# One-hot tiles of a gate expansion laid out as [token pair, key, 2] instead of [key, 8 tokens] in a one-core decoder trunk

## The chip, the cores and the metric

The kernel runs on one core of a Trainium2 chip. The metric is the device time of one execution in microseconds (us), from the first instruction to the last. The engines have short names in the rows: PE is the TensorE matmul, PEld its weight load, DVE the VectorE, ACT the ScalarE, POOL the GpSimd, SP the SyncE, which issues most of the transfers. Instructions of one engine run in the program's order; engines wait for each other by semaphores.

## What is computed

One decoder layer on 1024 tokens of width 1024, with 16 meta tokens in front: a convolution module beside latent attention, and then a mixer in which each of 8 heads picks, for each token, 16 of 16384 experts by a product of two key sets of 128 keys each. The mixer is what matters here:

```python
sv, si = lax.top_k(s, K)
cand = sv[:, :, 0, :, None] + sv[:, :, 1, None, :]
cidx = si[:, :, 0, :, None] * N_KEYS + si[:, :, 1, None, :]
top_s, sel = lax.top_k(cand.reshape(C, PEER_HEADS, K * K), K)
eidx = jnp.take_along_axis(cidx.reshape(C, PEER_HEADS, K * K), sel, axis=-1)
g = jax.nn.softmax(top_s, axis=-1)
u = u_tab[eidx]
act = jax.nn.gelu(jnp.einsum('chkd,cd->chk', u, xb).astype(jnp.float32), approximate=False)
w = (g * act).astype(xb.dtype)
return jnp.einsum('chk,chkd->cd', w, v_tab[eidx])
```

An expert's number is `i1 * 128 + i2`, with `i1` and `i2` the two keys. Each token has 8 x 16 = 128 (head, pick) pairs with a gate each.

## The kernel before

The tokens are cut into 8 chunks of 128. Input product, convolution and attention come first. For the mixer, four chunks (`GATHER`) fetch the rows of their experts by indirect transfers, and four (`DENSE`) go through all 16384 experts by matmul. A **gather step** of the first kind is 4 fetches `ug` (L687, issued by POOL) of 512 KB each into one of 3 buffers, and for each a DVE product with the tokens, `ujunk` (L690); of the second kind 4 fetches `vg` (L713) into 7 buffers, and 8 matmuls `gv` (L717).

The dense chunks need their gates as a table over all experts, `g_d`, in DRAM. `expand` (L738 to L764) makes it. For one dense chunk, the 128 (head, pick) pairs lie in the partitions, and the tile `gd` holds for each of 128 tokens the gate's high part (row 0) and low part (row 1), `i1` (row 2) and `i2` (row 3), all in 16-bit floats. The work goes in 4 blocks of 32 tokens, each block in 4 **batches** of 8 tokens (`TH`), so 64 batches in all. A batch has, on DVE, two comparisons of `gd` with the key numbers `io`, which give the one-hot tiles `two` (L749) and `one` (L750), the product `ah` (L751), and in batches 0 and 2 of a block also the product `al` (L752); in batches 1 and 3 POOL does `al` (`ALP`). Then PE does for each of the 8 tokens two matmuls (L756 with `ah`, L757 with `al`), each of which loads `two` as 128 x 128 weights and streams 128 columns, and adds them up in PSUM in `pg`. ACT copies `pg` out into `st` (L759), and SP writes a full `st` to `g_d` (L763). There is one buffer for `one`, and there are two each for `two`, `ah` and `al`.

What stands in memory: a tile of 128 x 128 x 8 two-byte elements with the token innermost. One token's 128 keys, which a matmul reads as its weights or its columns, therefore lie 16 bytes apart:

```python
one, two, ah, al = [ex.tile([P, NK, TH], F16, name=f"{n}{c}_{q}_{r0}", tag=n, bufs=b)
                    for n, b in (("one", 1), ("two", 2), ("ah", 2), ("al", 2))]
V.tensor_tensor(two, io, col(3), op=OP.is_equal)
PE.matmul(pg[:, k], two[:, :, r + k], ah[:, :, r + k], start=True, stop=False)
```

The order of the work: the code emits parts in the order of the string `ORDER`, and a scheduler then orders every engine's instructions by its own model of time. `E0` to `E3`, the expansions of the four dense chunks, run among the last selects (`S4`), the last product with `w_out` and the last query scores (`C4`), the transposed dense input (`N0`), the first three dense blocks (`U3`) and gather steps. After them comes the dense part (`dense`), with matmuls `pa` and `pv` (L178), in 32-bit format, 128 x 128 weights and 512 columns each. The last 128 gather steps run beside the dense part.

Of the kernel before, what the change touches and what calls it, by code (L numbers as in the profile page):

```python
# [16 lines left out]
F16 = mybir.dt.float16  # L17
# [3 lines left out]
OP = mybir.AluOpType  # L21
# [4 lines left out]
P = 128  # L26
D = 1024
KD = D // P
S = 1024
# [16 lines left out]
BIG = 3.0e38  # L46
# Pairs (a0, na, b0, nb) of sorted key scores that can be among the 16 (the first four: the 8) largest sums.
BLOCKS = [(0, 1, 0, 8), (1, 1, 0, 4), (2, 2, 0, 2), (4, 4, 0, 1),
# [8 lines left out]
WT = 512  # L57
# Emission order after the first chunk: B attention, C mix and query scores, S select, T turn of a token set;
# E gate expansion of a dense chunk, N transposed dense input, U dense blocks ahead, G gather steps, D the rest;
# X and Y hand the attention's and the mix's memory on.  # L60
ORDER = "B1 C1 S1 B2 C2 T1 S2 B3 C3 T2 S3 B4 X0 C4 T3 E0 E1 Y0 S4 T4 E2 N0 E3 U3 G32 D0"
# [21 lines left out]
def trunk_kernel(ctx, tc, x, meta, g_mix, w_ab, w_lat, g_q, w_uq, g_kv, w_ukv, conv_w, conv_b,  # L83
# [53 lines left out]
    def rsqrt(ms, name):  # L137
        """(ms + EPS) ** -0.5 of a [p, width] mean square, in place."""
        p, w = ms.shape
        G.tensor_tensor(ms, ms, pow_c[:p, 0, :w], op=OP.add)  # L140
        G.tensor_tensor(ms, ms, pow_c[:p, 1, :w], op=OP.pow)
        return ms
# [15 lines left out]
    def split_w(pool, ap, shape, name, bufs, eng):  # L158
        """Weight tile [P, nk, n] as an exact sum of two float32r parts."""
        nk, n = shape  # L160
        raw = pool.tile([P, WT], F32, name=name + "r", tag="wraw", bufs=4)
        hi = pool.tile([P, WT], F32R, name=name + "h", tag="whi", bufs=bufs)
        lo = pool.tile([P, WT], F32R, name=name + "l", tag="wlo", bufs=bufs)
        r, hh, ll = [t[:, :nk * n].rearrange("p (k n) -> p k n", n=n) for t in (raw, hi, lo)]
        nc.sync.dma_start(r, ap)
        A.activation(hh, r, AF.Copy)
        eng.tensor_tensor(ll, r, hh.bitcast(F32), op=OP.subtract)
        return hh, ll
# [11 lines left out]
    def to_T(src, m, XT, c0, k0=0, nk=KD, bank=bank):  # L180
        """Transposes rows src [m, nk * P] into the split pair XT at columns c0.."""
        for b in range(0, nk, 4):
# [18 lines left out]
    def phase_a():  # L201
        """Input norm, w_in product, conv module and the latent attention's projections; a generator that
        yields once the first chunk's part and everything that needs the transposed input is emitted."""
        ax_ctx, aw_ctx = ExitStack(), ExitStack()
# [35 lines left out]
        def project(j):  # L240
# [17 lines left out]
            def rope(dst, src, nh):  # L258
                """dst, src [m, nh, DR]"""
                co = cst[:m, None, :HF].broadcast_to([m, nh, HF])  # L260
# [11 lines left out]
            def headsT(src, dst_d, name):  # L272
                """src [m, H, DQ] -> dst_d [DQ, H, m]"""
                ht = pj.tile([DQ, H, P], F32, name=name, tag="hT", bufs=2)
                for b in range(2):
                    tq = bank("tq", tag="ap")
                    for q in range(4):
                        transpose_to(tq[:DQ, q * P:q * P + m], src[:m, 4 * b + q], m)
                    A.activation(ht[:, 4 * b:4 * b + 4, :m], tq.rearrange("p (k t) -> p k t", t=P)[:DQ, :, :m], AF.Copy)
                nc.scalar.dma_start(dst_d, ht[:, :, :m])  # L280
# [24 lines left out]
        def conv_v(b, c0, n, acc):  # L305
            """acc [P, n]: channel block b of the conv at tokens c0.."""
            for k in range(CK):
# [6 lines left out]
        def conv_g(b, c0, n, acc, pool):  # L314
            """The same with the products on ScalarE and the sums, in two chains, on GpSimd."""
            acc2 = pool.tile([P, n], F32, name=f"odd{b}_{c0}", tag=f"odd{n}", bufs=1)
# [97 lines left out]
    def attend_first():  # L414
        """Attention of the first chunk, four heads at a time."""
        qt = bp.tile([DQ, H, P], F32, name="qt0")
# [135 lines left out]
    def mix_out(si, MT):  # L552
# [5 lines left out]
        for nn in range(4):  # L558
            w = [load_w(cp, w_out[nn, :, 2 * kk:2 * kk + 2], (2, 256), f"wo{si}_{nn}_{kk}") for kk in range(4)]
            for j in range(nt):  # L560
# [4 lines left out]
                V.tensor_tensor(hv, hv, pb, op=OP.add)  # L565
# [1 line left out]
        NT = cp.tile([P, KD, dim.nw * P], F32, name=f"nt{si}", tag="mt", bufs=2)  # L567
        for j in range(nt):
# [5 lines left out]
            to_T(hs[j], P, NT, j * P)  # L574
# [1 line left out]
        sv = [sel.tile([P, H, 2, TK], F32, name=f"sv{si}_{j}", tag="sv", bufs=dim.nw) for j in range(nt)]  # L576
# [79 lines left out]
    def turn(c):  # L656
        """Expert indices (and gates) of chunk c with the (head, k) pairs in the partitions."""
        ef, g = picks[c]
# [17 lines left out]
    def gather_u(c):  # L676
        """Rows of u_tab against the tokens of chunk c; yields after every 4 (head, k) pairs."""
        g, ei = chunks[c][:2]
# [16 lines left out]
    def gather_v(c):  # L695
        """Weighted rows of v_tab for the tokens of chunk c; yields after every 4 tokens."""
        g, ei, eT = chunks[c]
# [40 lines left out]
    def expand(ci):  # L738
        """Dense gates of the DENSE tokens: g_d[i1 // NG, i2, t // TG, (i1 % NG, t % TG)]."""
        c = DENSE[ci]  # L740
        t = chunks[c]
        for q in range(P // TG):
            st = [ex.tile([P, NK // 2, TG], F32, name=f"st{c}_{q}_{i}", tag="st", bufs=STB) for i in range(2)]
            for r0 in range(0, TG, TH):
                def col(r):
                    return t[:, r, None, q * TG + r0:q * TG + r0 + TH].broadcast_to([P, NK, TH])
                one, two, ah, al = [ex.tile([P, NK, TH], F16, name=f"{n}{c}_{q}_{r0}", tag=n, bufs=b)
                                    for n, b in (("one", 1), ("two", 2), ("ah", 2), ("al", 2))]
                V.tensor_tensor(two, io, col(3), op=OP.is_equal)  # L749
                V.tensor_tensor(one, io, col(2), op=OP.is_equal)  # L750
                V.tensor_tensor(ah, one, col(0), op=OP.mult)  # L751
                (G if r0 // TH in ALP else V).tensor_tensor(al, one, col(1), op=OP.mult)  # L752
                for r in range(0, TH, 4):
                    pg = bank(f"pg{c}_{q}_{r0}_{r}", (P, 4, NK), "bs"[r // 4 % 2])
                    for k in range(4):
                        PE.matmul(pg[:, k], two[:, :, r + k], ah[:, :, r + k], start=True, stop=False)  # L756
                        PE.matmul(pg[:, k], two[:, :, r + k], al[:, :, r + k], start=False, stop=True)  # L757
                    for i in range(2):
# [128 lines left out]
    for step in ORDER.split():  # L887
# [11 lines left out]
        elif step[0] == "X":  # L899
            bp_ctx.close()  # L900
            ex = ex_ctx.enter_context(tc.tile_pool(name="ex", bufs=1, side="right", **RW))
            io = ex.tile([P, NK, TH], F16, name="io")
            G.iota(io, pattern=[[1, NK], [0, TH]], base=0, channel_multiplier=0, allow_small_or_imprecise_dtypes=True)
        elif step[0] == "Y":
# [22 lines left out]
def _layout(i):  # L927
# [3 lines left out]
    def blocks(w, n):  # L931
        """[D, M] -> [M / n, P, D / P, n]"""
        d, m = w.shape
        return c(w.reshape(d // P, P, m // n, n).transpose(2, 1, 0, 3))
# [43 lines left out]
```

## Time and profile before

| What | Value |
|---|---|
| Median of 3 runs | 3082.31 us (3082.04 to 3083.99) |
| Profiled execution, first to last instruction (its span, which is its time here) | 3090.9 us |
| Mean granted TensorE clock | 0.902 of full |
| Busy: PE / PEld / DVE / ACT / POOL | 2742.6 / 1995.1 / 2160.4 / 1022.9 / 1567.2 us |
| Moved by transfers | 858.36 MB, mean 278 GB/s |
| First and last matmul `pg` start at | 963.6 and 1435.6 us |

The profiled execution lies 8.6 us above the median. The chain of waits follows the work that ended last back to the start, and its shares say on what the end depended. A matmul's end in the rows is modelled, so the distance between the starts of two matmuls in a row says what one costs, and not its length. [...]

### The profile page before, as it was taken

How to read it: one execution, taken by the hardware profiler on the slowest of the kernel's cores; microseconds unless marked ns; L12 is line 12 of the kernel's file. 1: busy time of each engine (PE TensorE's matmuls, PEld its weight loads, DVE VectorE, ACT ScalarE, POOL GpSimd, SP SyncE). 2: the span in 40 equal slices, each digit the busy share in tenths (PEclk: the TensorE clock that was granted, in tenths of full speed). 3: DMA queues.
4: the chain of work that ended last, by engine and by line, in shares of the span. 5: the costliest groups of instructions: out<-in, count | busy, mean ns of one | idle time of the engine just before them, and what ended most of it. 6: DMA issues, size and time to landing. Idle time of an engine off the chain costs nothing.

```text
span 3090.9 us, 40498 instructions
## 1 busy us (share of the span) xinstructions
PE 2742.6 (89%) x13295; PEld 1995.1 (65%) x13295; DVE 2160.4 (70%) x4917; ACT 1022.9 (33%) x2200; POOL 1567.2 (51%) x1608
## 2 busy tenths in 40 slices
PE   7778578888876997887999899999999999999997
PEld 6765456766644654444877767777777777776664
DVE  4788957989988789855778776666666665653333
ACT  6445335443421333333322222322222222332222
POOL 5885443535568356654333354554455445434444
PEclk9898769988897776656999999999999999999999
DMA  4124689887788777879888899999999999988986
GB/s 156 33 59 146 215 271 314 271 260 227 242 312 295 244 262 237 276 253 304 291 281 292 286 353 336 334 355 339 333 354 335 345 324 351 333 322 313 325 305 225
DMA packets 372563, 858.36 MB, mean 278 GB/s; under 512 B 37952, under 2 KB 134400, under 8 KB 368256
## 3 DMA queue, kind: packets, MB, share of 16 engines
q0 software_dynamic: 147456, 536.94, 50.0%
q1 hardware_dynamic: 216528, 295.68, 28.4%
q10 hardware_dynamic: 8368, 23.15, 2.0%
q8 instruction: 105, 1.72, 0.2%
q14 instruction: 106, 0.87, 0.1%
HBM read 798.92 MB, written 56.71 MB: 277 GB/s over the span
## 4 chain that ended last, share of the span: by engine, by line
PE 58%; DVE 14%; DMA 11%; issue 5%; POOL 3%; ACT 1%; SPq 0%; another core or an unknown queue 0%; POOLq 0%; ACTq 0%; DVEq 0%
PE pa L178 19%; PE pv L178 19%; DMA ug<-in_dram,ei 8%; PE gv L717 7%; DVE ujunk L690 3%; PE pg L756 3%; PE pg L757 3%; PE q L583 3%; DVE ef L638 2%; DVE eq L636 1%; PE po L521 1%; POOL vg L713 1%; PE sp L493 1%; PE op L563 1%; DMA vg<-in_dram,eT 1%
## 5 line engine op out<-in xcount | busy, mean ns | idle before, releaser
L713 POOL DMA_INDIRECT vg<-in_dram,eT x512 | 556.6, 1087 | 682.7 <-PE gv L717 544.0
L687 POOL DMA_INDIRECT ug<-in_dram,ei x512 | 540.9, 1056 | 624.6 <-DVE ujunk L690 341.1
L690 DVE SCALAR_TENSOR_TENSOR ujunk<-ug,xn 128x1024 bf16<-128x1024 f32 x512 | 631.7, 1234 | 144.3 <-DMA ug<-in_dram,ei 137.0
L830 DVE TENSOR_TENSOR acc<-acc,pv 128x512 f32<-128x512 f32 x256 | 171.8, 684 | 213.2 <-PE pv L178 193.3
L717 PE MATMUL gv<-vg,wd 128*32 128x512 f32 x2048 | 278.0, 663 | 25.6 <-DMA vg<-in_dram,eT 25.6
L756 PE MATMUL pg<-ah,two 128*128 128x128 f16 x512 | 205.6, 414 | 41.7 <-DVE ah L751 39.6
L178 PE MATMUL pv<-v_0h,wh 128*128 128x512 f32 x512 | 203.1, 400 | 26.4 <-ACT wh L816 18.2
L759 ACT ACTIVATE st<-pg 128x256 f32<-128x256 f32 x256 | 140.0, 652 | 253.7 <-PE pg L757 228.1
L757 PE MATMUL pg<-al,two 128*128 128x128 f16 x512 | 204.7, 412 | 17.2 <-POOL al L752 15.8
L178 PE MATMUL pa<-xdh,u_1l 128*128 128x512 f32 x512 | 202.4, 395 | 2.4 <-DVE u_1l L779 2.4
L178 PE MATMUL pa<-xdh,u_0l 128*128 128x512 f32 x512 | 203.0, 396 | 0.2 <-DVE u_0l L779 0.2
L178 PE MATMUL pv<-v_1l,wh 128*128 128x512 f32 x512 | 200.5, 393 | 2.7 <-DVE v_1l L779 2.7
L178 PE MATMUL pa<-xdh,u_0h 128*128 128x512 f32 x512 | 202.9, 396 | 0.0
L178 PE MATMUL pa<-xdl,u_0h 128*128 128x512 f32 x512 | 202.1, 395 | 0.0
L178 PE MATMUL pa<-xdl,u_1h 128*128 128x512 f32 x512 | 201.6, 394 | 0.0
L178 PE MATMUL pv<-v_0l,wh 128*128 128x512 f32 x512 | 201.3, 396 | 0.0
L178 PE MATMUL pa<-xdh,u_1h 128*128 128x512 f32 x512 | 200.7, 392 | 0.0
L778 ACT ACTIVATE u_1h<-u_1r 128x512 fp32r<-128x512 f32 x128 | 80.7, 631 | 360.2 <-PE pa L178 268.9
L178 PE MATMUL pv<-v_1h,wl 128*128 128x512 f32 x512 | 199.5, 391 | 0.0
L178 PE MATMUL pv<-v_1h,wh 128*128 128x512 f32 x512 | 195.9, 394 | 1.8 <-DVE acc L830 1.8
L178 PE MATMUL pv<-v_0h,wl 128*128 128x512 f32 x512 | 194.0, 395 | 0.3 <-DVE wl L817 0.3
L778 ACT ACTIVATE u_0h<-u_0r 128x512 fp32r<-128x512 f32 x128 | 80.8, 631 | 310.6 <-PE pa L178 240.9
(449 smaller groups left out, 5932.1 us busy)
## 6 DMA issues: line engine op xcount, KB each, us to landing
g_d<-st SPq DMA_DIRECT2D x32, 1024.0 KB
u_0r<-in_dram SPq DMA_DIRECT2D x128, 256.0 KB
u_1r<-in_dram SPq DMA_DIRECT2D x128, 256.0 KB
gt<-g_d SPq DMA_DIRECT2D x32, 1024.0 KB
v_0r<-in_dram SPq DMA_DIRECT2D x128, 256.0 KB
v_1r<-in_dram SPq DMA_DIRECT2D x128, 256.0 KB
wo<-in_dram SPq DMA_DIRECT2D x80, 256.0 KB
wq<-in_dram SPq DMA_DIRECT2D x80, 256.0 KB
```

Source lines behind the costliest of these rows:

```text
L178: PE.matmul(dst, l, r, start=first and j == 0, stop=last and j == 2)
L583: PE.matmul(pb[:, :n], w[:, k], NT[:, kk + k, :n], start=kk + k == 0, stop=kk + k == KD - 1)
L638: V.tensor_reduce(e[:, h:h + HB, ks], pr.rearrange("p h c k -> p h k c"), axis=AX.X, op=OP.add)
L687: G.indirect_dma_start(out=ug, out_offset=None, in_=u_tab, in_offset=bass.IndirectOffsetOnAxis(ap=ei[:, j:j + 1], axis=0))
L690: V.scalar_tensor_tensor(junk, ug, 1.0, xn, op0=OP.mult, op1=OP.mult, accum_out=dots[:, j:j + 1])
L713: G.indirect_dma_start(out=vg[j], out_offset=None, in_=v_tab, in_offset=bass.IndirectOffsetOnAxis(ap=eT[:, t:t + 1], axis=0))
L717: PE.matmul(acc[32 * j:32 * j + 32, 512 * n:512 * n + 512], w[:, j, 32 * i:32 * i + 32], vg[j][:, 512 * n:512 * n + 512], start=q == 0 and ...
L756: PE.matmul(pg[:, k], two[:, :, r + k], ah[:, :, r + k], start=True, stop=False)
L757: PE.matmul(pg[:, k], two[:, :, r + k], al[:, :, r + k], start=False, stop=True)
L759: A.activation(st[i][:, :, r0 + r:r0 + r + 4].rearrange("p a b -> p b a"), pg[:, :, i * NK // 2:(i + 1) * NK // 2], AF.Copy, scale=1.0 / G ...
L778: A.activation(hi, raw, AF.Copy)
L830: V.tensor_tensor(a, a, pv, op=OP.add)
```

## The change

The four tiles get the shape [128, 4, 128, 2]: token pair, key, and the token within the pair innermost. One token's 128 keys now lie 4 bytes apart, not 16. `io` shrinks from [128, 8] to [128, 2] per partition and is read again for each pair, and the column operand `col` is read as runs of 2 elements, each run 128 times over, where it was a run of 8 read 128 times. The counts of instructions, their element counts and types, the matmuls' shapes, PSUM tiles, copies and transfers stay. Comments and docstrings are dropped as well.

```diff
             for r0 in range(0, TG, TH):
+                sh = [P, TH // 2, NK, 2]
+
                 def col(r):
-                    return t[:, r, None, q * TG + r0:q * TG + r0 + TH].broadcast_to([P, NK, TH])
-                one, two, ah, al = [ex.tile([P, NK, TH], F16, name=f"{n}{c}_{q}_{r0}", tag=n, bufs=b)
+                    cv = t[:, r, q * TG + r0:q * TG + r0 + TH].rearrange("p (a b) -> p a b", b=2)
+                    return cv[:, :, None, :].broadcast_to(sh)
+                one, two, ah, al = [ex.tile(sh, F16, name=f"{n}{c}_{q}_{r0}", tag=n, bufs=b)
                                     for n, b in (("one", 1), ("two", 2), ("ah", 2), ("al", 2))]
-                V.tensor_tensor(two, io, col(3), op=OP.is_equal)
-                V.tensor_tensor(one, io, col(2), op=OP.is_equal)
+                V.tensor_tensor(two, io[:, None].broadcast_to(sh), col(3), op=OP.is_equal)
+                V.tensor_tensor(one, io[:, None].broadcast_to(sh), col(2), op=OP.is_equal)
                 V.tensor_tensor(ah, one, col(0), op=OP.mult)
                 (G if r0 // TH in ALP else V).tensor_tensor(al, one, col(1), op=OP.mult)
...
-                        PE.matmul(pg[:, k], two[:, :, r + k], ah[:, :, r + k], start=True, stop=False)
-                        PE.matmul(pg[:, k], two[:, :, r + k], al[:, :, r + k], start=False, stop=True)
+                        a, b = divmod(r + k, 2)
+                        PE.matmul(pg[:, k], two[:, a, :, b], ah[:, a, :, b], start=True, stop=False)
+                        PE.matmul(pg[:, k], two[:, a, :, b], al[:, a, :, b], start=False, stop=True)
...
-            io = ex.tile([P, NK, TH], F16, name="io")
-            G.iota(io, pattern=[[1, NK], [0, TH]], base=0, channel_multiplier=0, allow_small_or_imprecise_dtypes=True)
+            io = ex.tile([P, NK, 2], F16, name="io")
+            G.iota(io, pattern=[[1, NK], [0, 2]], base=0, channel_multiplier=0, allow_small_or_imprecise_dtypes=True)
```

The scheduler also sets instructions of the expansions, and of what runs among them, in a somewhat different order from the start of `E0` on; ahead of that the order stays. In the changed file the lines of the batch are L752 to L755 and L760, L761. Two places are shown. The first is POOL in the last expansion, from the product `al` of block 1 (its last batch) to that of block 2; in the names, `al_2_8` is block 2 from token 8 on, and the numbers at the end are buffers. Before:

```order
L752 TENSOR_TENSOR al_1_24_11052<-one_1_24_11049,gd_10258 128x1024
L752 TENSOR_TENSOR al_2_8_11116<-one_2_8_11113,gd_10258 128x1024
L687 DMA ug_84_14090<-in_dram,ei_4618 128x1024
L687 DMA ug_85_14094<-in_dram,ei_4618 128x1024
L713 DMA vg_126_15046<-in_dram,eT_2889 128x1024
L713 DMA vg_31_15278<-in_dram,eT_2889 128x1024
L713 DMA vg_63_15280<-in_dram,eT_2889 128x1024
L713 DMA vg_95_15282<-in_dram,eT_2889 128x1024
L752 TENSOR_TENSOR al_2_24_11176<-one_2_24_11173,gd_10258 128x1024
```

And with the change:

```order
L755 TENSOR_TENSOR al_1_24_11052<-one_1_24_11049,gd_10258 128x1024
L687 DMA ug_85_14094<-in_dram,ei_4618 128x1024
L755 TENSOR_TENSOR al_2_8_11116<-one_2_8_11113,gd_10258 128x1024
L687 DMA ug_86_14098<-in_dram,ei_4618 128x1024
L713 DMA vg_127_15284<-in_dram,eT_2889 128x1024
L713 DMA vg_0_15373<-in_dram,eT_5632 128x1024
L687 DMA ug_87_14102<-in_dram,ei_4618 128x1024
L713 DMA vg_32_15375<-in_dram,eT_5632 128x1024
L755 TENSOR_TENSOR al_2_24_11176<-one_2_24_11173,gd_10258 128x1024
```

The fetches stand between the products in another order, and the stretch holds three fetches of each kind where it held two `ug` and four `vg`; by the last `al` of all, one `ug` and four `vg` more have been issued than before.

The second place is DVE at the same point, from the batch that starts at token 24 of block 1 into block 2. Before:

```order
L750 TENSOR_TENSOR one_1_24_11049<-io,gd_10258 128x1024
L751 TENSOR_TENSOR ah_1_24_11051<-one_1_24_11049,gd_10258 128x1024
L750 TENSOR_TENSOR one_2_0_11083<-io,gd_10258 128x1024
L749 TENSOR_TENSOR two_2_0_11084<-io,gd_10258 128x1024
L751 TENSOR_TENSOR ah_2_0_11085<-one_2_0_11083,gd_10258 128x1024
L752 TENSOR_TENSOR al_2_0_11086<-one_2_0_11083,gd_10258 128x1024
L749 TENSOR_TENSOR two_2_8_11114<-io,gd_10258 128x1024
L750 TENSOR_TENSOR one_2_8_11113<-io,gd_10258 128x1024
L690 SCALAR_TENSOR_TENSOR ujunk,dots_12008<-ug_81_14018,xn_12006 128x1024
L749 TENSOR_TENSOR two_2_16_11144<-io,gd_10258 128x1024
```

And with the change:

```order
L753 TENSOR_TENSOR one_1_24_11049<-io,gd_10258 128x1024
L754 TENSOR_TENSOR ah_1_24_11051<-one_1_24_11049,gd_10258 128x1024
L752 TENSOR_TENSOR two_1_24_11050<-io,gd_10258 128x1024
L690 SCALAR_TENSOR_TENSOR ujunk,dots_12008<-ug_82_14022,xn_12006 128x1024
L753 TENSOR_TENSOR one_2_0_11083<-io,gd_10258 128x1024
L754 TENSOR_TENSOR ah_2_0_11085<-one_2_0_11083,gd_10258 128x1024
L752 TENSOR_TENSOR two_2_0_11084<-io,gd_10258 128x1024
L755 TENSOR_TENSOR al_2_0_11086<-one_2_0_11083,gd_10258 128x1024
L752 TENSOR_TENSOR two_2_8_11114<-io,gd_10258 128x1024
L753 TENSOR_TENSOR one_2_8_11113<-io,gd_10258 128x1024
```

A product with a fetched row, `ujunk`, moves up by some five places, and `two` stands behind `ah` in two batches; the rule that `one` of the next batch follows the last reader of `one` on POOL or DVE stays.

## Rows read from the trace of the kernel before

**Rows 1.** The page: the span, and PE's clock in 40 slices of 77 us (tenths).

```profile
span 3090.9 us, 40498 instructions
...
PEclk9898769988897776656999999999999999999999
```

**Rows 2.** The page: the two groups of matmuls of the expansion (busy us, mean ns, idle before).

```profile
L756 PE MATMUL pg<-ah,two 128*128 128x128 f16 x512 | 205.6, 414 | 41.7 <-DVE ah L751 39.6
...
L757 PE MATMUL pg<-al,two 128*128 128x128 f16 x512 | 204.7, 412 | 17.2 <-POOL al L752 15.8
```

**Rows 3.** Busy time by stretch: start:end, length, PE, PEld, DVE, ACT, POOL, clock, DMA share, GB/s.

```profile
955.00:1110.00 155.00, 139.29 (x584) 90.01 (x586) 117.04 (x328) 46.19 (x93) 85.58 (x85) 0.80 0.76 259
1110.00:1260.00 150.00, 119.14 (x510) 68.69 (x503) 141.98 (x414) 49.63 (x94) 98.86 (x107) 0.70 0.75 249
1260.00:1436.00 176.00, 151.33 (x643) 78.86 (x644) 114.11 (x169) 68.76 (x127) 103.08 (x78) 0.57 0.84 276
1436.00:1810.00 374.00, 336.49 (x1441) 265.67 (x1441) 281.92 (x472) 104.73 (x185) 139.58 (x128) 0.96 0.86 296
1810.00:3090.00 1280.00, 1260.57 (x6188) 910.46 (x6186) 732.79 (x1175) 354.35 (x593) 601.71 (x563) 1.00 0.91 329
```

**Rows 4.** The chain of waits by line, in the first, second and third stretch of rows 3.

```profile
by line: PE q L583 19.4%; PE pg L756 18.3%; PE pg L757 18.2%; issue 5.9%; PE gv L717 4.9%; PE s L592 4.9%; POOL vg L713 4.1%; DVE ef L638 3.8%; POOL ep L637 3.6%; POOL cidx L619 3.5%; DVE ujunk L690 3.3%; DVE eq L636 2.7%; PE tp L156 2.2%; 
by line: PE pa L178 14.5%; PE pg L756 10.3%; PE pg L757 9.4%; DVE eq L636 7.6%; DVE ef L638 5.8%; DVE ujunk L690 4.6%; PE gv L717 4.5%; DMA xd<-xn_d 3.7%; DVE two L749 3.6%; DVE ah L751 3.6%; issue 3.3%; PE q L583 3.1%; DVE one L750 2.8%; D
by line: PE pg L757 24.6%; PE pg L756 23.6%; PE gv L717 14.1%; issue 11.0%; POOL al L752 7.2%; POOL vg L713 6.8%; DVE ah L751 4.7%; DVE two L749 2.0%; DVE ujunk L690 1.9%; POOL ug L687 1.9%; DVE one L750 1.4%; POOL ep L637 0.5%; ACT st L759
```

**Rows 5.** PE in order of time: `pg` around 1016 us, where 1.00 was granted.

```profile
1016.06 0.41 PE L757 MATMUL pg<-al,two 128*128 128x128 f16 x1
1016.29 0.41 PE L756 MATMUL pg<-ah,two 128*128 128x128 f16 x1
```

**Rows 6.** PE in order of time: `pg`, then `gv`, around 1310 us, where 0.50 was granted.

```profile
1309.49 0.41 PE L757 MATMUL pg<-al,two 128*128 128x128 f16 x1
1309.72 0.41 PE L756 MATMUL pg<-ah,two 128*128 128x128 f16 x1
...
1312.39 3.64 PE L717 MATMUL gv<-vg,wd 128*32 128x512 f32 x16
```

**Rows 7.** PE in order of time: `pv` and `gv` in the dense part, at clock 1.00.

```profile
1970.12 0.39 PE L178 MATMUL pv<-v_0h,wl 128*128 128x512 f32 x1
1970.35 0.39 PE L178 MATMUL pv<-v_0h,wh 128*128 128x512 f32 x1
...
1972.25 1.92 PE L717 MATMUL gv<-vg,wd 128*32 128x512 f32 x16
```

**Rows 8.** The weight loads of L757, all of them (busy us, mean ns).

```profile
L757 PEld LDWEIGHTS <-two 128*128 128x128 f16 x512 | 74.8, 146 | 51.4 <-issue 9.5
```

**Rows 9.** POOL in order of time through one block (start us, length us, wait before).

```profile
1305.21 2.72 POOL L752 TENSOR_TENSOR al<-one,gd 128x1024 f16<-128x1024 f16 x1 [5.16 <-DVE one L750]
...
1316.29 0.94 POOL L713 DMA_INDIRECT vg<-in_dram,eT  x1 [3.11 <-PE gv L717]
...
1320.96 1.91 POOL L752 TENSOR_TENSOR al<-one,gd 128x1024 f16<-128x1024 f16 x1
1327.86 2.72 POOL L752 TENSOR_TENSOR al<-one,gd 128x1024 f16<-128x1024 f16 x1 [4.98 <-DVE one L750]
```

**Rows 10.** DVE and POOL by line and shape, whole span: two-byte and four-byte operands.

```profile
L690 DVE SCALAR_TENSOR_TENSOR ujunk<-ug,xn 128x1024 bf16<-128x1024 f32 x512 | 631.7, 1234 | 144.3 <-DMA ug<-in_dram,ei 137.0 <-DMA xn<-xn_d 3.4 <-issue 2.1
...
L752 POOL TENSOR_TENSOR al<-one,gd 128x1024 f16<-128x1024 f16 x32 | 68.1, 2128 | 32.9 <-DVE one L750 31.0 <-PE pg L757 1.6
L637 POOL TENSOR_TENSOR ep<-eq,cidx 128x400 f32<-128x400 f16 x64 | 61.3, 958 | 17.2 <-DVE eq L636 16.3 <-DVE tv L603 0.4 <-issue 0.2
...
L749 DVE TENSOR_TENSOR two<-io,gd 128x1024 f16<-128x1024 f16 x64 | 52.1, 814 | 56.0 <-PE pg L757 55.7 <-issue 0.3
...
L750 DVE TENSOR_TENSOR one<-io,gd 128x1024 f16<-128x1024 f16 x64 | 44.5, 696 | 30.3 <-POOL al L752 30.1
```

## The prediction

> **What bounds the kernel now.** I read four views. The page first: of 40 slices those from the 10th to the 19th (about 700 to 1470 us) are where PE's clock is low [rows 1], and the expansions lie there. Then the busy time by stretch [rows 3], with cuts where the mix of work changes; the reader should compare in each row the fullest engine with the next. In the first stretch (955 to 1110 us) PE is fullest, 139.3 of 155 us, before DVE with 117.0. In the second (to 1260) it is DVE, 142.0 of 150, before PE with 119.1. In the third (to 1436), where hardly anything but the expansion and its gather steps runs, it is PE again, 151.3 of 176, DVE has 114.1, and the transfers' share is 0.84. In the fourth the chain runs through late fetches, and in the last PE is full at clock 1.00; neither has an expansion.
>
> Then the chain by line in the first three stretches [rows 4]: the matmuls of L756 and L757 are 36.5%, 19.7% and 48.2% of it, so 56.6, 29.5 and 84.8 us, 171 us in all, of 1024 matmuls [rows 2]. That is the most that could be touched.
>
> Last, PE in order of time: one `pg` matmul starts every 0.23 us, at clock 1.00 [rows 5] as at 0.50 [rows 6]. 1024 x 0.234 = 240 us. Something that halves its clock and keeps its pace is not limited by its own clock: the array waits for its operands. The dense part's matmuls on operands whose elements lie next to each other, 4 bytes apart, take the same 0.23 us for four times the columns [rows 7]. So 128 columns cost a quarter of that there, 57 ns at clock 1.00. At half clock I take the double, 113 ns: a group of 16 `gv` matmuls took 3.64 us at 0.50 [rows 6] and 1.92 us at 1.00 [rows 7].
>
> **The change, part by part.**
>
> *Matmuls.* Their two operands go from a pitch of 16 bytes to one of 4. No row shows two-byte elements at that pitch. Bounds: at worst the pace stays 234 ns. At best it is the dense row's: with the stretches' mean clocks of 0.80, 0.70 and 0.57 [rows 3], that is 40, 60 and 86% of the time at half clock, 79, 91 and 105 ns come out (0.4 x 113 + 0.6 x 57, and so on). Between lies 146 ns, if the weight load [rows 8] kept its length and became the limit. I take the best price, since its row has just this pitch, and has a weight load to every matmul in the last stretch [rows 3] as `pg` has. The relief per matmul is then 155, 143 and 129 ns, for 256, 256 and 512 matmuls: 40, 37 and 66 us of PE's time.
>
> *First stretch.* PE falls to 139.3 - 40 = 100 us, and DVE with 117.0 is fullest. PE now fills 0.90 of the stretch; filling as much, DVE needs 117.0 / 0.90 = 130 us. **Minus 25 us.**
>
> *Second stretch.* DVE is fullest before and after, with 8 us idle. I take half of these: **minus 4 us.** What remains is DVE's selects beside the comparisons.
>
> *Third stretch.* A block of 4 batches takes 1327.86 - 1305.21 = 22.65 us on POOL [rows 9]. Two waits in it hang on PE: 3.11 us until `gv`, which PE does behind a batch of `pg`, and about 5 us before the first `al`, in which DVE makes two batches' tiles and waits for the second buffer of `two`. The first goes when a batch of 16 matmuls shrinks from 3.7 to 1.7 us. Of the second, six DVE operations of some 0.62 us stay, 3.7 us. So the ring is 22.65 - 3.1 - 1.3 = 18.2 us, and what is late next is POOL itself: two `al`, three `ug`, four `vg`, with `ujunk` between them. That would make 141 us of the stretch. But the transfers' time, 0.84 x 176 = 148 us, does not shrink: 148 us if they were never idle, 154 us if they filled 0.96. I take 151: **minus 25 us.** With the weight load's 146 ns instead the ring loses the first wait all the same, and with 116 us PE is no longer fullest in the first stretch, so that the three together would still be about 40 us.
>
> *DVE and POOL operations.* Element counts and types stay. I take nothing for them, since each operand still has neighbouring two-byte elements innermost, only in shorter runs. Bounds: nothing better; at worst a DVE operation costs what 1024 elements cost on four-byte operands, 1234 instead of 690 to 810 ns [rows 10] (a rival below). For POOL's `al` the other row per element is 958 / 400 = 2.4 ns [rows 10], so 2.45 us against a mean of 2.13, at two in a block 0.6 of 18.2 us, 5 us over the third stretch; it does not show here whether that would hold for short runs.
>
> *The smaller `io`* is one POOL operation, ahead of the first batch; nothing. *The new order:* by the last `al` one `ug` and four `vg` more are issued than before, so the fourth stretch has slightly less left. At its pace that is some us at most; I leave it at nothing, and in the range. Transfers and PSUM copies are the same in number and size. ACT, with 68.8 of 176 us, waits for PE and follows.
>
> *Later stretches.* They shift forward as they are: the gather steps are paced there by their own three buffers, and the dense matmuls by PE.
>
> **Sum:** 25 + 4 + 25 = 54 us off a profiled 3090.9 us, so 3037. The profiled execution lies 8.6 us above the median of 3082.3; against the median I forecast **3028 us**.
>
> **The rivals.**
>
> *All of the chain's share comes back.* If nothing else is late in the place of `pg`, the chain's 56.6, 29.5 and 84.8 us shrink by 155, 143 and 129 in 234: 37 + 18 + 47 = 102 us, 2980 us. For it: the chain goes through `pg` there and not through transfers. Against: DVE's 142 of 150 us in the second stretch, and the transfers' 0.84 in the third.
>
> *The clock takes part of it back.* The granted clock went with PE's load here: 1.00 where PE was full, 0.80 in the first stretch at 90%, 0.57 in the third at 86% [rows 3]. PE's other work in the first stretch is 139.3 - 60 = 79 us; at 0.57 in place of 0.80 it is 111 us, with 27 us of `pg` 138 us, so 153 us at the same filling: that stretch then gives back 23 of its 25 us and the total is 3051. Against: a stream that waits for operands at every column may count for less than its busy time, and then a denser stream raises the clock. [...]
>
> *The third stretch is held by its transfers.* The gates' table and the fetches move at 276 GB/s at a share of 0.84 there; if 0.84 is all this mix gives, that stretch gains nothing and the total is 3082 - 29 = 3053 us. Against: the last stretch holds 0.91 over 1280 us.
>
> *The pace of `pg` is not that of its pitch.* Then it stays at 234 ns, the tiles are as good as the old ones, and the time is 3080 us. For it: no row varies the pitch alone. Against: matmuls with four times the columns run at the same pace. [...]
>
> *Slower: DVE loses its pairs.* At 690 ns a two-byte operation handles two elements in the time in which `ujunk` handles one. If runs of two in `col` ended that, 224 operations cost 0.53 us more each: 30, 30 and 59 us. DVE then has 147, 172 and 173 us; at fillings of 0.90, 0.947 (now) and 0.95 the stretches take 163, 181 and 182 us, against 155, 150 and 176: 45 us slower, 3127 us. It decides from about 0.35 us more per operation on. No row has such short runs. [...]
>
> **How the numbers follow.** Forecast 0.38; all of the chain 0.24; the clock 0.13; the transfers 0.09; no effect of the pitch 0.07; DVE slower 0.09. Over 0.2% is over 6 us, about what a measurement of this kernel can tell from no change: the first four are faster, 0.84, the fifth is the same, 0.07, the last slower, 0.09. The range takes in the first four, with 10 us more at the low end, for the fourth stretch's lighter load, and 13 us at the high end, for `al` and a dearer matmul: 2970 to 3066. It leaves out 0.16.
>
> **What would show it.** In the changed profile `pg` starts should lie 60 to 115 ns apart, and further apart at half clock than at full. The three stretches should take some 130, 146 and 151 us, with DVE fullest in the first two, and on POOL the waits for `gv` gone. The comparisons should still take about 0.69 us, `al` about 2.1 us. Wrong it would be if the first `pa` of the dense part came forward and the end did not, if DVE's operations took 1.2 us, or if the pace of `pg` stayed at 234 ns.

## The result, and the profile after

The changed kernel took 3033.82 us (median of 4 runs, 3022.82 to 3034.39), the kernel before, measured beside it, 3082.65 us (3082.04 to 3083.99): a ratio of 0.9842 (95% interval 0.982 to 0.9864), 49 us less. The profiled execution of the change is the lowest of its four, 3022.8 us with a span of 3021.0.

The page of the changed kernel answers to [rows 1, 2]; the last line is a group of matmuls (busy us, mean ns, idle before):

```profile
span 3021.0 us, 40497 instructions
...
PEclk9888859898898877667999999999999999999999
...
L760 PE MATMUL pg<-ah,two 128*128 128x128 f16 x512 | 97.1, 269 | 82.7 <-DVE ah L754 60.2
```

The clock is low in the same slices as before, the 13th to the 19th, a little less so, and a group of `pg` has 97.1 us of busy time in place of 205.6. PE in order of time (start us, length us) shows the pace, first where 1.00 was granted, then at 0.50:

```profile
1022.73 0.22 PE L761 MATMUL pg<-al,two 128*128 128x128 f16 x1
1022.78 0.22 PE L760 MATMUL pg<-ah,two 128*128 128x128 f16 x1
1022.84 0.22 PE L761 MATMUL pg<-al,two 128*128 128x128 f16 x1
...
1287.34 0.31 PE L760 MATMUL pg<-ah,two 128*128 128x128 f16 x1
1287.45 0.31 PE L761 MATMUL pg<-al,two 128*128 128x128 f16 x1
1287.55 0.31 PE L760 MATMUL pg<-ah,two 128*128 128x128 f16 x1
```

Over all `pg` the median from start to start is 57 ns at 1.00 and 107 ns at 0.50; before, it was 234 ns at both [rows 5, 6].

For the stretches I cut both traces at the same work: from the last `po` of the attention (L521) to the 17th of the 64 batches, to the 33rd, to the last `pg`. Busy time by stretch before (columns as in [rows 3]):

```profile
895.00:1112.30 217.30, 175.46 (x745) 109.78 (x744) 173.07 (x572) 51.89 (x107) 134.64 (x144) 0.78 0.76 256
1112.30:1263.20 150.90, 116.84 (x498) 68.39 (x495) 142.88 (x408) 48.84 (x92) 101.76 (x109) 0.70 0.76 252
1263.20:1435.60 172.40, 150.93 (x642) 78.36 (x642) 110.91 (x165) 68.76 (x127) 99.88 (x75) 0.57 0.84 274
```

And after:

```profile
885.60:1077.00 191.40, 129.86 (x761) 88.46 (x761) 175.27 (x574) 48.14 (x108) 138.69 (x149) 0.84 0.88 304
1077.00:1218.80 141.80, 74.97 (x497) 46.00 (x496) 138.84 (x407) 44.90 (x89) 106.62 (x108) 0.70 0.78 261
1218.80:1375.50 156.70, 82.92 (x641) 51.36 (x639) 109.50 (x162) 64.55 (x130) 101.41 (x76) 0.63 0.94 308
```

The three are 25.9, 9.1 and 15.7 us shorter, 50.7 us in all (540.6 to 489.9). The rest of the difference between these two executions can't be put down to the change: 9.4 us had come about by the last `po`, before any changed instruction, and the part after the last `pg` (1655.3 to 1645.5) lay between 1637 and 1661 us in all the kernels run. So below I compare the time from the last `po` to the last `pg`, beside the ratios.

In the first two stretches DVE is now the fullest engine by far. In the third nothing is full: PE 83, DVE 110, POOL 101 of 157 us, and the transfers at a share of 0.94. What the engines wait for there (us, times, longest), before:

```profile
DVE one L750 <- POOL al L752: 30.1, 5, 7.2
...
POOL vg L713 <- PE gv L717: 17.0, 7, 4.6
```

And after:

```profile
PE pg L761 <- POOL al L755: 39.5, 10, 6.1
DVE one L753 <- POOL al L755: 38.3, 8, 6.5
...
POOL al L755 <- DVE one L753: 17.9, 6, 4.1
...
POOL vg L713 <- PE gv L717: 10.7, 5, 3.4
```

DVE and POOL wait for each other. POOL in order of time through one block shows how, the answer to [rows 9]:

```profile
1300.77 2.72 POOL L755 TENSOR_TENSOR al<-one,gd 128x1024 f16<-128x1024 f16 x1 [3.90 <-DVE one L753]
...
1308.88 1.26 POOL L713 DMA_INDIRECT vg<-in_dram,eT  x1 [1.69 <-PE gv L717]
...
1315.35 1.90 POOL L755 TENSOR_TENSOR al<-one,gd 128x1024 f16<-128x1024 f16 x1
1321.35 2.71 POOL L755 TENSOR_TENSOR al<-one,gd 128x1024 f16<-128x1024 f16 x1 [4.10 <-DVE one L753]
```

And DVE at the same place:

```profile
1300.52 1.22 DVE L690 SCALAR_TENSOR_TENSOR ujunk<-ug,xn 128x1024 bf16<-128x1024 f32 x1
...
1301.66 2.37 DVE L754 TENSOR_TENSOR ah<-one,gd 128x1024 f16<-128x1024 f16 x1
...
1310.09 0.69 DVE L754 TENSOR_TENSOR ah<-one,gd 128x1024 f16<-128x1024 f16 x1
1317.28 0.69 DVE L753 TENSOR_TENSOR one<-io,gd 128x1024 f16<-128x1024 f16 x1 [6.49 <-POOL al L755]
```

DVE has made the tiles of a batch by 1310.8 and needs the one buffer of `one` back. POOL's `al`, which reads it, stands in POOL's queue behind seven issues of fetches, until 1315.35; DVE is idle for 6.5 us. Then POOL waits 4.1 us until DVE has made the next batch. From one such `al` to that of the next block this one takes 20.6 us; the seven of the stretch take 16.9 to 21.5 us, mean 19.0. Before, the seven took 19.0 to 23.9 us, mean 21.3.

DVE's and POOL's operations kept their length by the median. Duration (min/median/max, ns), before:

```profile
L749 DVE TENSOR_TENSOR two<-io,gd x64: 661/692/2607, 959.1 to 1423.5; 128x1024 f16<-128x1024 f16 x64
...
L752 POOL TENSOR_TENSOR al<-one,gd x32: 1884/1909/2909, 975.6 to 1430.2; 128x1024 f16<-128x1024 f16 x32
```

And after:

```profile
L752 DVE TENSOR_TENSOR two<-io,gd x64: 665/684/2382, 942.2 to 1367.7; 128x1024 f16<-128x1024 f16 x64
...
L755 POOL TENSOR_TENSOR al<-one,gd x32: 1892/1904/2739, 963.0 to 1372.1; 128x1024 f16<-128x1024 f16 x32
```

### The profile page after: what moved, and what is told of

The parts are those of the page before. It is cut to its first block, busy times and chain, and to the rows that moved or that the text cites. A ratio compares the mean times of both kernels' runs of the same rounds, so it can differ in the third digit from the quotient of the medians.

```text
span 3021.0 us, 40497 instructions
## 1 busy us (share of the span) xinstructions
PE 2592.5 (86%) x13295; PEld 1928.7 (64%) x13295; DVE 2158.9 (71%) x4917; ACT 1010.7 (33%) x2200; POOL 1572.4 (52%) x1608
## 5 line engine op out<-in xcount | busy, mean ns | idle before, releaser
L713 POOL DMA_INDIRECT vg<-in_dram,eT x512 | 563.0, 1100 | 635.7 <-PE gv L717 504.3
L690 DVE SCALAR_TENSOR_TENSOR ujunk<-ug,xn 128x1024 bf16<-128x1024 f32 x512 | 640.6, 1251 | 144.2 <-DMA ug<-in_dram,ei 140.8
L763 ACT ACTIVATE st<-pg 128x256 f32<-128x256 f32 x256 | 128.6, 646 | 200.7 <-PE pg L761 157.7
L783 DVE TENSOR_TENSOR u_0l<-u_0r,u_0h 128x512 fp32r<-128x512 f32 x128 | 90.0, 703 | 118.6 <-ACT u_0h L782 114.6
L760 PE MATMUL pg<-ah,two 128*128 128x128 f16 x512 | 97.1, 269 | 82.7 <-DVE ah L754 60.2
```

Source lines behind the costliest of these rows:

```text
L690: V.scalar_tensor_tensor(junk, ug, 1.0, xn, op0=OP.mult, op1=OP.mult, accum_out=dots[:, j:j + 1])
L713: G.indirect_dma_start(out=vg[j], out_offset=None, in_=v_tab, in_offset=bass.IndirectOffsetOnAxis(ap=eT[:, t:t + 1], axis=0))
L760: PE.matmul(pg[:, k], two[:, a, :, b], ah[:, a, :, b], start=True, stop=False)
L763: A.activation(st[i][:, :, r0 + r:r0 + r + 4].rearrange("p a b -> p b a"), pg[:, :, i * NK // 2:(i + 1) * NK // 2], AF.Copy, scale=1.0 / G ...
L783: V.tensor_tensor(lo, raw, hi.bitcast(F32), op=OP.subtract)
```

## The experiments

Twelve kernels ran, in three groups of four; the kernel before ran beside each group, with medians of 3079.83, 3085.77 and 3083.41 us, and ratios are to those. Every edit can give the scheduler another order of all engines' instructions, which is a second change that no diff shows. Two kernels are said to have the same order here when in the traces, by operation and names, every instruction on POOL, PE and SP stands at the same place, and on DVE (4917 instructions) and ACT (2258) all but five at most. Where no such thing is said, the order is another.

### What the pace of the matmuls depends on

**Old tiles, dense reads.** The kernel before, whose matmuls read 128 elements that lie next to each other.

```diff
-  PE.matmul(pg[:, k], two[:, :, r + k], ah[:, :, r + k], start=True, stop=False)
+  f2, fh, fl = [x.rearrange("p k t -> p (k t)")[:, (r + k) * NK:(r + k + 1) * NK] for x in (two, ah, al)]
+  PE.matmul(pg[:, k], f2, fh, start=True, stop=False)
```

> DVE, POOL and the tiles are those of the kernel before; only the matmuls of the expansion read 128 neighbouring elements (pitch 2 bytes) instead of every eighth. They so read other elements than a token's keys, and the gates' table has other values. Theory A (the pitch at which PE reads is the whole of it): pg starts 55 to 60 ns apart at clock 1.00 and about 107 at 0.50, time 3034 us within 12. Rival B (the layout on DVE and POOL, or the order the scheduler made of it, brings a good part): above 3055 us.

Measured: 3036.22 us, ratio 0.9852 (0.9825 to 0.9879), and 487.3 us from the last `po` to the last `pg`. `pg` starts 56 ns apart at full and 107 ns at half clock, here the latter:

```profile
1281.80 0.31 PE L758 MATMUL pg<-al,two 128*128 128x128 f16 x1
1281.90 0.31 PE L757 MATMUL pg<-ah,two 128*128 128x128 f16 x1
```

Its order is that of before. The read pitch by itself gives the whole gain: the three stretches take 192.1, 143.2 and 152.0 us, so 25.2, 7.7 and 20.4 less than before.

**New tiles, old reads.** The changed kernel with the opposite edit: its matmuls read every eighth element, 16 bytes apart, out of the new tiles.

> The changed tiles, made in runs of two, but the matmuls read them at a pitch of 16 bytes as before (other elements than a token's keys, so the table has other values). Theory A: pg 234 ns apart at either clock, time 3083 us within 10. Rival B: below 3065 us, with the pace of 234 ns. Should DVE or POOL pay for the short runs, it shows here: above 3095 us.

Measured: 3082.93 us, 1.0006 (0.9992 to 1.0019), 541.2 us, `pg` 234 ns apart at either clock:

```profile
1281.15 0.41 PE L762 MATMUL pg<-al,two 128*128 128x128 f16 x1
1281.39 0.41 PE L761 MATMUL pg<-ah,two 128*128 128x128 f16 x1
```

It has the change's order. So the new shape of DVE's and POOL's operations and the new order, taken together at the old pace, bring nothing and cost nothing. Its stretches take 217.3, 148.8 and 175.2 us; against them the change gains 25.9, 7.0 and 18.5.

**Weights only, and columns only.** In the first `two` has the new layout and `one`, `ah` and `al` the old; in the second it is the other way round.

```diff
-  PE.matmul(pg[:, k], two[:, a, :, b], ah[:, a, :, b], start=True, stop=False)
+  PE.matmul(pg[:, k], two[:, a, :, b], ah[:, :, r + k], start=True, stop=False)
```

```diff
-  PE.matmul(pg[:, k], two[:, a, :, b], ah[:, a, :, b], start=True, stop=False)
+  PE.matmul(pg[:, k], two[:, :, r + k], ah[:, a, :, b], start=True, stop=False)
```

> Only two, the tile that is loaded as weights, has the new layout (4 bytes); one, ah and al, the streamed columns, keep 16 bytes. If the stream of columns set the pace: weight loads near 105 ns, pg still 234 ns apart, time 3083 us within 10. If the weight load set it: pg at 57 and 107 ns, 3034 us. If both are read one after the other: in between, near 170 ns and 3050 us.

> The reverse of the run in which only the weights were dense: one, ah and al in the new layout (columns 4 bytes apart), two in the old one (weights 16 bytes apart); the values are the reference's. Theory A (the streamed columns set the pace, and the weight load lies beside the stream): pg starts 57 to 107 ns apart as in the change and 3034 us, within 8 us. Rival B (weights at 16 bytes need about 146 ns a load, as before the change, and that becomes the pace): about 146 ns per matmul at either clock, and, with the first stretch still on DVE, 3034 to 3050 us.

Measured: weights only 3074.84 us, 0.9981 (0.9966 to 0.9997), `pg` 229 ns apart at either clock, with weight loads of 121 ns, not 105; columns only 3018.77 us, 0.9787 (0.977 to 0.9803). PE in order of time in the kernel with dense columns only, at full clock:

```profile
1021.48 0.22 PE L762 MATMUL pg<-ah,two 128*128 128x128 f16 x1
1021.54 0.23 PE L763 MATMUL pg<-al,two 128*128 128x128 f16 x1
1021.61 0.23 PE L762 MATMUL pg<-ah,two 128*128 128x128 f16 x1
```

and its weight loads, by line (busy us, mean ns):

```profile
L763 PEld LDWEIGHTS <-two 128*128 128x128 f16 x512 | 73.0, 154 | 25.6 <-issue 25.1
```

A weight load of 154 ns by its record lies beside a stream that starts a matmul every 63 ns (107 at half clock): the streamed columns set the pace, and beside the change's 57 ns the weights' pitch costs 6 ns at full clock. The pace is theory A's, the time is not: it lies 15 us under the 3034 us expected. The weights are not what makes this kernel faster than the change, since its matmuls cost a little more. Its order is another, that of weights only, which at the old pace was worth next to nothing (0.9981).

**Pitch of 32 bytes.** The kernel with dense weights only, with `ah` and `al` in tiles twice as wide.

```diff
-  ah, al = [ex.tile([P, NK, TH], F16, name=f"{n}{c}_{q}_{r0}", tag=n, bufs=2) for n in ("ah", "al")]
+  ah, al = [ex.tile([P, NK, 2 * TH], F16, name=f"{n}{c}_{q}_{r0}", tag=n, bufs=2) for n in ("ah", "al")]
-  V.tensor_tensor(ah, one, col8(0), op=OP.mult)
+  V.tensor_tensor(ah[:, :, :TH], one, col8(0), op=OP.mult)
```

> The streamed operands ah and al with their elements 32 bytes apart (tiles twice as wide, every second group of 8 unused), two as in the change, one as before; the values are the reference's. It measures the price of the pitch by itself: 16 bytes took 229 to 234 ns for 128 columns, 8 bytes 118 ns, 4 bytes 57 ns at full clock. Theory A (the price goes with the distance from element to element): 460 to 470 ns per pg matmul at either clock; 240 us more of PE in the expansions, which end some 150 to 230 us later: 3230 to 3310 us. Rival B (the price goes by 16-byte pieces touched, one per column from 16 bytes on): 229 to 234 ns as at 16 bytes, and about 3075 to 3085 us.

Measured: 3085.57 us, 1.0001 (0.9987 to 1.0015), `pg` 233 ns apart at either clock:

```profile
1331.52 0.41 PE L762 MATMUL pg<-ah,two 128*128 128x128 f16 x1
1331.75 0.41 PE L763 MATMUL pg<-al,two 128*128 128x128 f16 x1
1331.98 0.41 PE L762 MATMUL pg<-ah,two 128*128 128x128 f16 x1
```

Rival B holds: from 16 bytes to 32, the distance costs nothing more. This kernel and the one with dense columns only have the same order too, and between them lie 66.8 us.

**Quads.** The change with four tokens innermost in place of two: [token quad, key, 4], a pitch of 8 bytes.

```diff
-  sh = [P, TH // 2, NK, 2]
+  sh = [P, TH // 4, NK, 4]
```

> Tiles as [token quad, key, 4], a pitch of 8 bytes, and col in runs of four. [...] If each element costs by its distance: pace near 115 ns at both clocks, and 3034 to 3055 us.

Measured: 3019.94 us, 0.9799 (0.9764 to 0.9834); 118 ns from start to start at full clock and at half:

```profile
1299.71 0.30 PE L761 MATMUL pg<-al,two 128*128 128x128 f16 x1
1299.83 0.30 PE L760 MATMUL pg<-ah,two 128*128 128x128 f16 x1
1299.95 0.30 PE L761 MATMUL pg<-al,two 128*128 128x128 f16 x1
```

The pace is the one expected "if each element costs by its distance", which the pitch of 32 bytes, above, limits to distances up to 16 bytes; the time lies under the 3034 to 3055 us expected with it. Matmuls that cost twice the change's at full clock give a time at least as good. At half clock, where more than half of `pg` runs, 118 stands against 107 ns, and DVE is fullest in the first two stretches, so that PE's further relief need not show there. This kernel has another order than the change, so no run shows this by itself.

### What sets the third stretch now

**Half the matmuls.** The change with one matmul per token.

```diff
-  PE.matmul(pg[:, k], two[:, a, :, b], ah[:, a, :, b], start=True, stop=False)
-  PE.matmul(pg[:, k], two[:, a, :, b], al[:, a, :, b], start=False, stop=True)
+  PE.matmul(pg[:, k], two[:, a, :, b], (ah if b else al)[:, a, :, b], start=True, stop=True)
```

> The changed kernel with one matmul per token where there were two (a token of odd number in its pair takes ah, one of even number al; the other product, so half of each sum of the table, is left out). Everything else is kept. It asks whether PE still sets the length of the expansions. Theory A (the relief is used up: DVE sets the first two stretches, transfers and POOL's ring the third): 512 matmuls fewer bring nothing more, 3034 us as the changed kernel, within 8 us, and the third stretch keeps its 157 us. Rival B (pg is still in the chain of every batch, as the rival in which all of the chain's share comes back would have it): 8 matmuls less per batch, 0.46 us at full and 0.86 us at half clock, on 64 batches: 30 to 50 us less, about 2990 us.

Measured: 3023.31 us, 0.9794 (0.9777 to 0.981). Its third stretch:

```profile
1229.90:1366.00 136.10, 56.24 (x384) 28.33 (x383) 112.22 (x156) 60.56 (x125) 98.40 (x71) 0.61 0.99 340
```

The first two stretches (193.0 and 144.6 us) gained nothing, as theory A has it; the third lost 20.6 us, as rival B has it for its 32 batches. So PE still has a part in what sets the third stretch, or the other order of this kernel has; the run alone does not part these. It does show that the mix can move at a share of 0.99.

**Half the table.** Only the first `st` is written, and the dense part reads that half twice.

```diff
-  nc.sync.dma_start(g_d[gs, :, ci * (P // TG) + q].rearrange("g p r -> p g r"),
-                    st[i].rearrange("p (g a) t -> p g (a t)", a=NG))
+  if i == 0:
+      nc.sync.dma_start(g_d[gs, :, ci * (P // TG) + q].rearrange("g p r -> p g r"),
+                        st[i].rearrange("p (g a) t -> p g (a t)", a=NG))
...
-  nc.sync.dma_start(gt.rearrange("p a b c -> p a (b c)"), g_d[g])
+  nc.sync.dma_start(gt.rearrange("p a b c -> p a (b c)"), g_d[g % (NK // NG // 2)])
```

> The changed kernel, with half of the gates' table left out: only the first of the two st halves is written to DRAM, and the dense part reads that half twice, so that it reads as many bytes as before. 16.8 MB of writes less in the expansions, about 8.4 MB of them in the third stretch, which moved 308 GB/s x 157 us = 48 MB at a share of 0.94. Theory A (transfers set the third stretch now): it falls from 157 us to what is late next, POOL's ring of 18 to 20 us a block, so to 140 to 150 us, and the total to about 3015 to 3025 us. Rival B (the ring of DVE and POOL sets it, and the share of 0.94 comes along with it): the stretch keeps 157 us, the share falls to some 0.80, and the total stays within 6 us of 3034 us.

Measured: 3036.23 us, 0.9847 (0.9828 to 0.9866). Its third stretch:

```profile
1236.90:1392.70 155.80, 73.31 (x593) 50.91 (x592) 141.55 (x193) 62.15 (x128) 107.32 (x80) 0.58 0.81 267
```

6.7 MB less were moved there (267 x 155.8 against 308 x 156.7), the share is 0.81, the stretch is as long, and the total is rival B's. But its reason is not shown. In this kernel's order 38 `ug` are issued in the stretch in place of 24, and DVE has 141.6 of 155.8 us to do, not 109.5 of 156.7. DVE is nearly full, and the wait that rival B speaks of is almost gone:

```profile
DVE one L753 <- POOL al L755: 6.6, 3, 2.8
```

So the run does not say what sets the stretch in the changed kernel. That transfers had room there is shown by other rows: half the matmuls moved 46.3 MB at a share of 0.99, and every `al` on DVE, below, 49.3 MB in 141.3 us, more than the change's 48.3 MB in 156.7.

**The change again, two buffers for `one`, every `al` on DVE.** Three kernels measured side by side.

> The changed kernel itself, with no edit, so that the other three kernels of this call stand beside it on one chip. In the first measurement it took 0.9842 of the time before, in the calls since, its variants took between 0.9787 and 0.9852. If what separates them is their order and edits, it is at 0.983 to 0.986 again, 3030 to 3040 us; if it is the chip and the hour, it may be as low as 0.979 beside them, 3019 us.

```diff
-  for n, b in (("one", 1), ("two", 2), ("ah", 2), ("al", 2))]
+  for n, b in (("one", 2), ("two", 2), ("ah", 2), ("al", 2))]
```

> The changed kernel with two buffers for one in place of one. Theory A (the third stretch is a ring of DVE and POOL through the single buffer of one: DVE waits 38 us there for POOL's al, POOL 18 us for DVE's one): both waits go, the blocks of 17 to 21 us fall to about 16, the third stretch from 157 us to 140 to 148, and the total by 8 to 15 us against the change in the same call. Rival B (transfers, at a share of 0.94): other waits take their place, the stretch stays at 150 to 157 us and the total within 6 us of the change.

```diff
-ALP = [1, 3]
+ALP = []
```

> The changed kernel with every al on DVE, none on POOL: 32 products of 0.68 us more on DVE (5, 5 and 11 us in the three stretches), 61 us less on POOL. Theory A (DVE is fullest in the first two stretches, and the pair of DVE and POOL sets the third): the first two grow by some 5 us each, the third falls by about 10 as the exchange between the two engines goes; all in all within 8 us of the change. Rival B (DVE sets all three): 22 us or more longer, 3056 us. Rival C (POOL is what all three wait for): 20 us or more shorter.

Measured: the change again 3043.68 us, 0.9853 (0.9832 to 0.9875), with stretches of 194.2, 142.2 and 155.4 us, within 3 us of its first profile. Two buffers for `one`: 3012.28 us, 0.9762 (0.9748 to 0.9777), stretches of 187.8, 127.2 and 148.7 us; in the third, DVE's wait for POOL's `al` falls from 38.3 us in the change:

```profile
DVE one L753 <- POOL al L755: 15.7, 5, 4.0
```

Every `al` on DVE: 2999.49 us, 0.9721 (0.9703 to 0.9739), 44 us less than the change beside it. Its stretches:

```profile
896.40:1073.00 176.60, 122.13 (x725) 82.51 (x725) 161.30 (x526) 45.90 (x101) 128.67 (x137) 0.82 0.89 308
1073.00:1200.40 127.40, 77.22 (x492) 49.59 (x489) 121.14 (x421) 46.02 (x93) 81.05 (x89) 0.71 0.86 292
1200.40:1341.70 141.30, 79.94 (x684) 53.77 (x683) 124.95 (x209) 63.95 (x132) 77.74 (x73) 0.72 1.00 349
```

and what ACT and PE wait for in the third:

```profile
ACT st L763 <- DMA g_d<-st: 40.8, 11, 5.2
...
PE pg L760 <- ACT st L763: 34.7, 8, 9.3
```

For two buffers the total fell by 31 us, more than theory A had, and less of it where A looked for it: 6.7 us in the third stretch and 15.0 in the second. The cut is at the same batches, but the order moved other work across it: the second stretch holds 425 of PE's matmuls where the change has 498, the third 717 where it has 639. For `al` on DVE my theory A (within 8 us) was wrong, and the number is rival C's, with all three stretches shorter. That POOL held up all three fits, and is not shown by itself. DVE has 32 products more, some 22 us, and yet less busy time in the three stretches, 407 against 418 us in the change beside it. The transfers look like the limit of the third only now: their share is 1.00, and ACT waits for a written `st`. Both kernels have other orders than the change too, so what part of 31 and 44 us is the exchange between DVE and POOL and what part is order is not settled. Together the two edits were not tried.

**Dense columns only, two buffers for `one`.** The same edit on the kernel with dense columns only.

> The run with dense columns alone (0.9787 of the time before) with two buffers for one. Theory A (the ring through one): 5 to 12 us less than that run, a ratio of 0.975 to 0.977, about 3010 us. Rival B (its third stretch, 140 us at a share of 0.96, is full of transfers): the same ratio, 0.978 to 0.981.

Measured: 3017.17 us, 0.978 (0.9762 to 0.9797), the ratio of rival B but not its reason: the second stretch fell from 140.1 to 120.8 us, the first and third rose from 188.7 to 194.9 and from 139.6 to 149.7. Inconclusive: with another order the gain of one stretch was given back in two.

## Why the prediction was right, point by point

**The bound and the price** held. The array waited for its operands: taking the pitch away in the old tiles gave 0.9852, keeping it in the new ones 1.0006. The first has the order of the kernel before and the second that of the change, so the order has no part in it. The price of 57 and 113 ns was taken from rows on four-byte operands at a 4-byte pitch; 57 and 107 ns were measured. The shares of the time at half clock took a mean clock for a mix of 1.00 and 0.50: each of the 122 clock records in the trace before, and of the 118 after, holds one of these two. The weight load, named as the possible limit at 146 ns, lies beside the stream: with dense columns only, a load took 154 ns and a matmul started every 63. One reading was off: the page's low clock begins at the 13th slice, where the expansions do, and not at the 10th; nothing hangs on it.

**First stretch**, minus 25 forecast: minus 25.9 measured (23.1 in the second profile of the change), and 25.2 with dense reads in the old order. DVE is fullest there, as said.

**Second stretch**, minus 4: minus 9.1 (8.7). The step that shared DVE's 8 idle us in half was too careful: 3 us are idle now, and DVE's own time fell from 142.9 to 138.8. With the order held the same it is 7.0 and 7.7.

**Third stretch**, minus 25: minus 15.7 (17.0), and 18.5 to 20.4 with the order held the same. This is the term that was mis-sized. "The transfers' time, 0.84 x 176 = 148 us, does not shrink" led me to 151 us. In the change that time is 147 us (0.94 x 156.7), as said, but it is no floor: it is 141 us in the kernel with every `al` on DVE, which moves more. The stretch is longer than the transfers need, and what the rows show in their place is DVE and POOL waiting for each other in a ring that did not shrink as far as I had it. The one block that I followed, 22.65 us, was longer than most: the mean of seven was 21.3. I brought it to 18.2; the mean is 19.0. So a block lost 2.3 us and not 4.4. The waits for `gv` on POOL, which I took off, are not gone: 17.0 us in the third stretch before, 10.7 after, 1.3 a block. And a wait that I did not look at is DVE's: 38.3 us for an `al` that stands behind the issues of fetches, 30.1 us before the change. That this ring alone sets the stretch is read from these waits, and no run isolates it; whether PE still has a part in it stays open.

**The sum** was closer than its terms, and that was luck: the second stretch gave 5 us more than forecast, the third 9 less, and 50.7 us came out for 54.

**DVE and POOL operations, order, later stages** at nothing: right. The comparisons have medians of 684 ns (`two`) and 682 (`one`), and had 692 and 681 before, so the runs of two keep their pairs and that rival is out. The new order with the old pace gave 1.0006.

**The clock** did not take the gain back. With a quarter to almost a half less busy time on PE, the granted clock went from 0.78 to 0.84, 0.70 to 0.70 and 0.57 to 0.63. Had it gone with the busy time, as the rival has it, it would have fallen, and it did not. Why it did not stays open. The rival's own reading, that the clock went with PE's load before, also leaves out the second of [rows 3], where PE was busy for 79% and 0.70 was granted, more than the 0.57 at 86% in the third.

**All of the chain's share**, 2980 us, did not come back in the change, since DVE and POOL were late next. 2999 us with every `al` on DVE says that more was to be had once POOL was relieved; how much of it is that share, and how much another order, is not shown.

## What to carry to other kernels

Lay out what a matmul streams so that neighbouring columns lie at most 4 bytes apart (128 columns took 57 ns at full clock so, 118 at 8 bytes, 234 at 16); when a matmul keeps its pace while its clock halves, look at the pitch of its streamed operand first, and at that of the weights last (here 0.9787 with dense columns only, 0.9981 with dense weights only). Then ask what the next ring is and follow it on every engine in it: an operation shared out to POOL stood behind fetch issues there, and a kernel with it back on the fuller engine, DVE, gained nearly as much as the layout had, in an order that was new as well. And compare edits with the order in mind: three orders that took 3075 to 3086 us with the old pace took 3019 to 3044 us with the new one.

## What the runs showed of the hardware that was not expected

**A streamed operand at a pitch of 8 bytes cost half of one at 16, and one at 32 as much as at 16, each the same at either clock.** 128 two-byte columns took 233 ns at a pitch of 32 bytes, 234 at 16 and 118 at 8. Counted by the 16-byte pieces of memory that they span, with one, one and two columns in each, that is 1.82, 1.83 and 1.84 ns a piece; the count is mine, and the runs show the paces alone. At half clock these three stay. At 4 bytes it is 57 ns at full clock and 107 at half, so the step from 8 bytes to 4 halved the price once more at full clock. Columns that lie next to each other took 56 and 107: below 4 bytes 1 ns came off at full clock, and nothing at half.

**Some of the expansion's DVE operations took up to 2.98 us, where 0.68 is their median, beside an `al` on POOL, and ended just after it.** In the rows above `ah` starts at 1301.66 while `al` runs on POOL until 1303.49, and ends at 1304.03, 2.37 us long where 0.69 is usual; `al` itself started under `ujunk` and took 2.72 in place of 1.90. In the profile of before, 15 of the expansion's DVE operations, 0.86 to 2.98 us long, ended 0.55 to 0.56 us after an `al` on POOL, in that of the change 7. What in the chip links the two is not shown. With every `al` on DVE, 4 of the expansion's operations on DVE took over 0.9 us, in the change 14: that fits the busy time DVE did not gain there, though it is not all of it. It is not what held the change up, or not alone: with two buffers for `one`, 20 operations end so, and that kernel is 31 us faster.
